# Feed-forward input products as seven half products, narrower matmuls, and a second mixer with wide products

## Chip, cores and metric

One core of a Trainium2 chip. The metric is the device time of one execution in microseconds. Three runs of the kernel before took 1454.93, 1454.94 and 1455.49 us; the time is their median, 1454.94 us.

## The reference

Two layers of a speech encoder over 384 tokens (256 frames of one stream, 16 of each of 8 later streams), width 1024, feed-forward width 2816, all in float32:

```python
def _swiglu(x, w_in, w_down):
    gate, up = jnp.split(x @ w_in, 2, axis=-1)
    return (jax.nn.silu(gate) * up) @ w_down

def _post_norm(x, sub, g, b):
    return _layer_norm(DEEPNORM_ALPHA * x + sub, g, b)

x <- LN(alpha*x + 0.5*SwiGLU_1(x)); x <- LN(alpha*x + Mixer(x)); x <- LN(alpha*x + 0.5*SwiGLU_2(x))
```

The mixer of the first layer is chunked attention with 16 heads and a relative bias; that of the second is windowed attention with 16 query heads on 4 key heads, rotary positions and one learned sink per head, which stands in the denominator of the softmax. There are four feed-forwards, two in each layer.

## The kernel before

**Products in three passes.** A float32 matrix is held as a high part and a remainder, both in the matmul's rounded float32 type: `split` (L68 to L70) casts the high part on ScalarE (L69) and subtracts on VectorE (L70). `mm3` (L119 to L122) multiplies high by high, high by low and low by high, so a product costs three matmuls. The lines L120, L121 and L122 below are these three.

**Weights.** All weights pass once through a ring of 8 tiles of 128x1024 (`ring_h`, `ring_l`), in the order that `Weights` (L72) is given. `ahead` (L97) issues a DMA on SP into a raw tile and splits it as soon as the ring has a free place; `take` hands out the next tile and `done` (L115) frees it. `first` (L78) brings the first four tiles in slabs, while dummy matmuls on zeros (`warm`, L952 to L955) run ahead of the first product.

**Tokens.** `x` holds the tokens in rows; `xh`, `xl` hold them transposed (features on partitions) and split, for three blocks of 128 tokens. `to_xT` (L130) transposes a block on TensorE with `ident` (L134) and splits it out of the bank; `layer_norm` (L145) makes a block of `x`: a sum with the old `x` (L150), statistics (L153), the normalised value (L165 to L169).

**A feed-forward** (`ffn`, L200) goes over 22 chunks of 128 hidden features. `in_chunk` (L211) makes one chunk: a gate tile and an up tile of weights, 8 blocks of 128 input features each, three matmuls for a block, 128 weight columns against all 384 tokens. Then SiLU and product (L208, L209) and the split of the hidden state. After each chunk from the third on, `down` (L271) adds the chunk two before it to the output: 6 steps (3 token blocks by 2 halves of the output) of three matmuls with 512 columns. The last 4 chunks' `down` steps come at the end, block by block, so that the layer norm of a block runs beside the next block's. The first two chunks are special: `opening` (L280) in the first feed-forward, elsewhere `first_chunks` (L229), which takes the tokens as the stationary operand, needs four weight tiles at once, and handles block by block, so that it can start before the last block is normalised. `ffn_order` (L184) lists the weight tiles in this order.

**The mixers** use a small planner, `Flow` (L339), which puts attention units between the products by their length, room in banks and what they need. `Mixer.natural` (L519) makes products with the tokens stationary: `natural(512)` with 512 weight columns, `natural(256)` with 256. In the second mixer (`mixer_b`, L692) there is one product of 512 and four of 256. It loads its sinks (L704, L707) and their negatives (L712, L714) at its own start.

## Time and profile before

| | |
|---|---|
| median of three runs | 1454.94 us |
| the profiled execution: time, span | 1457.14 us, 1455.4 us |
| granted TensorE clock over the span | 0.997 |
| TensorE matmuls (PE) | 1439.5 us, 99%, 8302 matmuls |
| TensorE weight loads (PEld) | 1298.8 us, 89% |
| VectorE (DVE), ScalarE (ACT), GpSimd (POOL) | 683.2, 543.9, 43.9 us |
| data moved by DMA | 203.81 MB, mean 140 GB/s |

How to read it: a busy time is the union of an engine's instruction durations. Matmuls overlap: the profile gives a 384-column matmul 0.34 us, while the next one starts 0.17 us after it, so the price of a matmul in a stream is the distance between starts. The weight load of a matmul is a row of its own (PEld) and runs beside the matmul before. "[5.16 <-DVE x L169]" behind a row means that the engine stood idle for 5.16 us ahead of it, until VectorE's instruction of L169 ended.

### The profile page before, as it was taken

Reading aid. Unit: us, or ns where it says so; the run is one execution under the profiler, and the core shown is the slowest. Engines: PE = TensorE matmul, PEld = TensorE weight load, DVE = VectorE, ACT = ScalarE, POOL = GpSimd, SP = SyncE. Lnnn points to the kernel's source line nnn. Section 1 sums busy time; section 2 is a strip of 40 time slices with the busy share of each in tenths; the row PEclk is TensorE's granted clock in tenths of the full one; section 3 lists DMA queues with packets and bytes.
Section 4 is the critical chain, followed back from the end, with each engine's and each line's share of the span. In section 5 each row is a group of like instructions: output and inputs, shape, how many; then the busy total and the mean of one; then the engine's idle time right before and its main releaser. Section 6 shows DMA issues by size and latency. Waiting matters only on the chain.

```text
span 1455.4 us, 20664 instructions
## 1 busy us (share of the span) xinstructions
PE 1439.5 (99%) x8302; PEld 1298.8 (89%) x8302; DVE 683.2 (47%) x1119; ACT 543.9 (37%) x989; POOL 43.9 (3%) x77
## 2 busy tenths in 40 slices
PE   9999999999999999999999999999899999999997
PEld 8999999897887899999989999999797789999996
DVE  6433333754356633333374333334776674333334
ACT  6333233355564433333323333332256453323320
POOL 0000000100000000000000000000210000000001
PEclk9999999999999999999999999999999999999999
DMA  8733333266845533333334333333441054333321
GB/s 291 273 130 131 118 128 130 95 216 199 274 150 155 186 125 130 130 119 127 130 102 161 129 130 127 120 130 130 148 154 43 15 190 144 130 121 126 131 87 44
DMA packets 69455, 203.81 MB, mean 140 GB/s; under 512 B 7228, under 2 KB 20160, under 8 KB 69232
## 3 DMA queue, kind: packets, MB, share of 16 engines
q1 hardware_dynamic: 63856, 188.24, 38.7%
q0 software_dynamic: 3200, 10.85, 2.3%
q10 hardware_dynamic: 2304, 3.41, 0.6%
q8 instruction: 65, 1.06, 0.3%
q14 instruction: 30, 0.25, 0.1%
HBM read 196.56 MB, written 5.24 MB: 139 GB/s over the span
## 4 chain that ended last, share of the span: by engine, by line
PE 97%; DMA 1%; ACT 1%; DVE 1%; issue 0%; POOL 0%; DVEq 0%; ACTq 0%
PE bank L120 30%; PE bank L122 30%; PE bank L121 30%; PE bank L651 1%; PE bank L134 1%; DMA sinkpb<-in_sinks 1%; PE bank L627 1%; PE bank L893 1%; PE bank L796 0%; PE bank L835 0%; PE bank L453 0%; PE bank L955 0%; PE bank L824 0%; PE bank L426 0%; DMA raw<-in_w_in 0%; PE bank L463 0%
## 5 line engine op out<-in xcount | busy, mean ns | idle before, releaser
L70 DVE TENSOR_TENSOR ring_l<-raw,ring_h 128x1024 fp32r<-128x1024 f32 x312 | 381.3, 1224 | 497.9 <-ACT ring_h L69 497.2
L69 ACT CAST ring_h<-raw 128x1024 fp32r<-128x1024 f32 x312 | 326.7, 1049 | 713.6 <-PE bank L121 417.8
L120 PE MATMUL bank<-xh,ring_h 128*128 128x384 f32 x1440 | 485.1, 337 | 0.0
L122 PE MATMUL bank<-xh,ring_l 128*128 128x384 f32 x1440 | 482.3, 335 | 0.0
L121 PE MATMUL bank<-xl,ring_h 128*128 128x384 f32 x1440 | 481.6, 334 | 0.0
L120 PEld LDWEIGHTS bank<-xh,ring_h 128*128 128x128 f32 x1440 | 270.5, 188 | 5.4 <-issue 1.2
L121 PEld LDWEIGHTS bank<-xl,ring_h 128*128 128x128 f32 x1440 | 270.5, 188 | 3.8 <-DVE xl L70 0.5
L122 PEld LDWEIGHTS bank<-xh,ring_l 128*128 128x128 f32 x1440 | 270.3, 188 | 0.0
L122 PE MATMUL bank<-ring_h,hl 128*128 128x512 f32 x528 | 209.0, 396 | 0.0
L120 PE MATMUL bank<-ring_h,hh 128*128 128x512 f32 x528 | 208.9, 396 | 0.0
L121 PE MATMUL bank<-ring_l,hh 128*128 128x512 f32 x528 | 207.6, 393 | 0.0
L209 DVE TENSOR_TENSOR hf<-sg,bank 128x384 f32<-128x384 f32 (+1 forms) x91 | 49.2, 540 | 182.4 <-PE bank L122 164.2
L120 PE MATMUL bank<-ring_h,xh 128*128 128x512 f32 (+1 forms) x336 | 125.9, 375 | 0.0
L122 PE MATMUL bank<-ring_h,xl 128*128 128x512 f32 (+1 forms) x336 | 122.0, 364 | 0.7 <-DVE ve L157 0.7
L121 PE MATMUL bank<-ring_l,xh 128*128 128x512 f32 (+1 forms) x336 | 121.3, 361 | 0.0
L122 PEld LDWEIGHTS bank<-ring_h,hl 128*128 128x128 f32 x528 | 99.2, 188 | 24.0 <-DVE hl L70 1.0
L121 PEld LDWEIGHTS bank<-ring_l,hh 128*128 128x128 f32 x528 | 99.6, 189 | 19.6
L120 PEld LDWEIGHTS bank<-ring_h,hh 128*128 128x128 f32 x528 | 99.5, 188 | 19.4
L120 PEld LDWEIGHTS bank<-ring_h,xh 128*128 128x128 f32 x336 | 63.7, 190 | 12.8 <-issue 3.5
L122 PEld LDWEIGHTS bank<-ring_h,xl 128*128 128x128 f32 x336 | 63.6, 189 | 11.3 <-DVE ve L157 1.1
L121 PEld LDWEIGHTS bank<-ring_l,xh 128*128 128x128 f32 x336 | 63.8, 190 | 8.1 <-issue 0.2
L159 POOL TENSOR_TENSOR rstd<-ve,mhalf 128x1 f32<-128x1 f32 x18 | 17.6, 979 | 1249.1 <-DVE ve L157 1249.1
(171 smaller groups left out, 805.7 us busy)
## 6 DMA issues: line engine op xcount, KB each, us to landing
raw<-in_w_in SPq DMA_DIRECT2D x172, 512.0 KB, 3.2
raw<-in_w_down SPq DMA_DIRECT2D x88, 512.0 KB, 3.2
kta<-in_kT_a SPq DMA_DIRECT2D x16, 512.0 KB, 6.2
vca<-in_v_a SPq DMA_DIRECT2D x16, 512.0 KB, 5.6
raw<-in_w_qk_a SPq DMA_DIRECT2D x16, 512.0 KB, 3.4
raw<-in_w_v_a SPq DMA_DIRECT2D x8, 512.0 KB, 3.4
raw<-in_w_o_a SPq DMA_DIRECT2D x8, 512.0 KB, 5.9
raw<-in_w_kv_b SPq DMA_DIRECT2D x8, 512.0 KB, 3.7
```

What stands on the lines that cost most here:

```text
L69: nc.scalar.copy(hi, src)
L70: nc.vector.tensor_tensor(lo, src, hi.bitcast(F32), op=ALU.subtract)
L120: nc.tensor.matmul(out, lh, rh, start=first, stop=False)
L121: nc.tensor.matmul(out, lh, rl, start=False, stop=False)
L122: nc.tensor.matmul(out, ll, rh, start=False, stop=last)
L134: nc.tensor.transpose(out=pt[:, j * P:(j + 1) * P], in_=x[:, t, (4 * h + j) * P:(4 * h + j + 1) * P], identity=ident,)
L159: nc.gpsimd.tensor_tensor(rstd, ve, mhalf, op=ALU.pow)
L209: nc.vector.tensor_tensor(hf, sg, up, op=ALU.mult)
L627: nc.tensor.matmul(pk[32 * j:32 * j + 32, 0:n], qbd[:, 4 * g + j, b, :], kt[:, j, :], start=True, stop=True)
L651: nc.tensor.matmul(po[32 * j:32 * j + 32, 0:P], pT[:, w] if i < 2 else pT[0:DS, w], vc[:, i, d] if i < 2 else vn[:, d], start=(i == 0), st ...
L893: nc.tensor.matmul(po[w, i, :], vn[:, b + i, d] if l else vc[:, b + i, d], pT[0:DS, u] if l else pT[:, u], start=(l == 0), stop=(l == 1),)
```

## The change

**Half products.** From the fifth chunk on (18 of 22 in each feed-forward) the two products of a chunk (gate and up, 1024 input features by 384 tokens) are taken as a product of 2 by 2 blocks: weights A11 (gate, first 512 input features), A12 (gate, last 512), A21 and A22 (up); tokens B in first and last 512 features, and in the first and the last 64 tokens of each block of 128. Instead of eight block products of 512 features by 128 hidden features by 192 tokens there are seven (the scheme of Strassen and Winograd), on sums of blocks: S1 = A21 + A22, S2 = S1 + A11, S3 = A11 + A21, S4 = S2 + A12 (plain sums; the signs are in the token combinations and in the factor -1 of `gated_half`). `Chunk.make` forms a sum on VectorE and splits it into a half unit of the ring; `combine` forms the four token combinations of a block of 128 tokens once per feed-forward (`ch`, `cl`), for the first two blocks at the transposes, for the last in `combine_late`, after a GpSimd sum of its two parts. Two banks X and Y of 192 columns collect the products; ScalarE copies three intermediate results out (`kept`), VectorE adds them (`summed`).

**Ring and order.** The ring holds the same bytes in 16 units of 512 columns, a full tile takes two. A chunk in the new form takes seven units. The order of a feed-forward is padded to a multiple of 16 units, 6 here. In a chunk A11, A12, S2, S1, S3, A22, S4 have single down steps between them (`STEPS`), as many as the hidden states made so far allow.

**Small edits.** WARM goes from 3 to 2. `load_sinks` moves the sinks out of `mixer_b`, behind the gate that the ninth chunk of the first feed-forward opens. `mixer_b` makes its keys, values and queries by three products of 512 columns (`w_qkv_b`). The tokens' first transposed copy, `xTf`, lies in the space of `x`.

```diff
-RING = 8
+RING = 16
+UNIT = 512
+PLAIN = 4
+HQ = 64
...
-WARM = 3
+WARM = 2
...
+    ring_h = xp.tile([P, RING, UNIT], F32R, name="ring_h")
+    ring_l = xp.tile([P, RING, UNIT], F32R, name="ring_l")
...
+    class Chunk:
...
+        def make(self, name, hi, lo):
+            def add(out, p, q):
+                nc.vector.tensor_tensor(out, p, q, op=ALU.add)
+            if name == "A11":
+                raw = W.pairs.tile([P, 4, UNIT], F32, name="pair")
+                for s in range(2):
+                    nc.sync.dma_start(raw[:, 2 * s:2 * s + 2, :].rearrange("p a f -> p (a f)"), self.src[s])
+                self.a11, self.a12, self.a21, self.a22 = (raw[:, i, :] for i in range(4))
+                self.s1 = W.pairs.tile([P, UNIT], F32, name="s1")
+                split(self.a11, hi, lo)
+                add(self.s1, self.a21, self.a22)
+            elif name == "A12":
+                split(self.a12, hi, lo)
+                self.s3 = self.a21
+                add(self.s3, self.a11, self.a21)
+            elif name == "S2":
+                self.s2 = self.a11
+                add(self.s2, self.s1, self.a11)
+                split(self.s2, hi, lo)
+            elif name == "S1":
+                split(self.s1, hi, lo)
+            elif name == "S3":
+                split(self.s3, hi, lo)
+            elif name == "A22":
+                split(self.a22, hi, lo)
+            else:
+                add(self.a12, self.s2, self.a12)
+                split(self.a12, hi, lo)
...
+                u = us.start % RING
+                if chunk:
+                    job[0].make(job[1], ring_h[:, u, :], ring_l[:, u, :])
+                elif not isinstance(job, int):
+                    raw = wr.tile([P, 1024], F32, name="raw")
+                    nc.sync.dma_start(raw, job)
...
+            if comb:
+                if h == 0:
+                    xf = comb[0][2].tile([P, KC, P], F32, name="xf")
+                nc.scalar.copy(xf[:, 4 * h:4 * h + 4, :].rearrange("p k q -> p (k q)"), pt)
+        if comb:
+            combine(xf[:, 0:4, :], xf[:, 4:8, :], t)
+        else:
+            late.append(t)
...
+    def combine_late():
+        while late:
+            t = late.pop(0)
+            xf = comb[0][2].tile([P, KC, P], F32, name="xf")
+            nc.gpsimd.tensor_tensor(xf, xh[:, t].bitcast(F32), xl[:, t].bitcast(F32), op=ALU.add)
+            combine(xf[:, 0:4, :], xf[:, 4:8, :], t)
+    def combine(b1, b2, t):
+        ch, cl, _ = comb[0]
+        b11, b12, b21, b22 = b1[:, :, 0:HQ], b1[:, :, HQ:P], b2[:, :, 0:HQ], b2[:, :, HQ:P]
+        nc.vector.tensor_tensor(b11, b11, b12, op=ALU.subtract)
+        nc.vector.tensor_tensor(b12, b22, b12, op=ALU.subtract)
+        nc.vector.scalar_tensor_tensor(b22, b11, -1.0, b22, op0=ALU.mult, op1=ALU.subtract)
+        nc.vector.scalar_tensor_tensor(b21, b22, -1.0, b21, op0=ALU.mult, op1=ALU.subtract)
+        for i, f in enumerate((b11, b22, b12, b21)):
+            split(f, ch[:, i, :, t, :], cl[:, i, :, t, :])
...
+    STEPS = ("A11", "A12", None, "S2", "S1", None, "S3", None, None, "A22", "S4", None)
+    def ffn_plan(layer, which):
...
+            chunk = Chunk((layer, which), w_in[j, 0], w_in[j, 1])
+            left = (n - 2 * NT * (PLAIN - 2)) * (j - PLAIN + 1) // (NF - PLAIN) + 2 * NT * (PLAIN - 2) - set_
+            set_ += left
+            for i, name in enumerate(STEPS):
+                if name:
+                    steps.append((j, (chunk, name)))
+                elif left:
+                    steps.append(next(downs))
+                    left -= 1
+            steps += [next(downs) for _ in range(left)]
...
+        order += [w_down[j] for j in range(NF - NTAIL, NF)]
+        n = sum(1 if isinstance(o, tuple) else 2 for o in order)
+        return order + ([-n % RING] if n % RING else [])
...
+            def chunk_step(j, name):
+                if name == "A11":
+                    hv["x"], hv["y"] = bank()[:, 0:T // 2], bank()[:, 0:T // 2]
+                    hv["hf"] = tp.tile([P, T], F32, name="hf")
+                    hv["sg"] = tp.tile([P, 2, T // 2], F32, name="sg")
+                    hv["up"] = tp.tile([P, T // 2], F32, name="up")
+                    hs[j] = hp.tile([P, T], F32R, name="hh"), hp.tile([P, T], F32R, name="hl")
+                X, Y, sg, up = hv["x"], hv["y"], hv["sg"], hv["up"]
+                hf = halves(hv["hf"])
+                out = Y if name in ("A11", "S2", "S3", "A22") else X
+                wn = W.take()
+                hi, lo = W.half(wn, 0)
+                for k in range(KC // 2):
+                    f = slice(k * P, (k + 1) * P)
+                    if name in ("S1", "S2", "S3", "A22"):
+                        i = ("S1", "S2", "S3", "A22").index(name)
+                        rh, rl = (c[:, i, k].rearrange("p t q -> p (t q)") for c in comb[0][:2])
+                        ov = out
+                    else:
+                        kk, q = (k, 0) if name == "A11" else (k + 4, 0) if name == "A12" else (k + 4, HQ)
+                        rh, rl = (c[:, :, kk, q:q + HQ] for c in (xh, xl))
+                        ov = out.rearrange("p (t q) -> p t q", q=HQ)
+                    mm3(
+                        ov, hi[:, f], lo[:, f], rh, rl, k == 0 and name in ("A11", "A12", "S1"),
+                        k == KC // 2 - 1, partial=True,
+                    )
+                W.done(wn)
+                def kept(name):
+                    b = tp.tile([P, T // 2], F32, name=name)
+                    nc.scalar.copy(b, Y)
+                    hv[name] = b
+                def gated_half(i, u):
+                    nc.vector.scalar_tensor_tensor(
+                        hf[:, i], u.rearrange("p (t q) -> p t q", q=HQ), -1.0,
+                        sg[:, i].rearrange("p (t q) -> p t q", q=HQ), op0=ALU.mult, op1=ALU.mult,
+                    )
+                def summed(out, kept):
+                    nc.vector.tensor_tensor(out, X, hv[kept], op=ALU.add)
+                if name == "A11":
+                    kept("p1")
+                elif name == "A12":
+                    summed(sg[:, 0], "p1")
+                    nc.scalar.activation(sg[:, 0], sg[:, 0], AF.Silu)
+                elif name == "S2":
+                    kept("u2")
+                elif name == "S3":
+                    kept("u3")
+                    summed(up, "u3")
+                elif name == "A22":
+                    gated_half(0, Y)
+                elif name == "S4":
+                    summed(sg[:, 1], "u2")
+                    nc.scalar.activation(sg[:, 1], sg[:, 1], AF.Silu)
+                    gated_half(1, up)
+                    split(hv["hf"], hs[j][0], hs[j][1])
...
+                combine_late()
                 next(fc)
-            for j in range(2, NF):
-                in_chunk(j)
-                if first and j < 2 + NT:
...
+    def load_sinks():
...
+            m.natural(512, take_q, first=True)
+            m.natural(512, take_kv, whole=True)
...
-            for c in (4, 6):
-                acc = m.natural(256)
-                for t in range(NT):
-                    flow.waiting.insert(t, (set(), {"qr": 1}, queries((2, 0, 1)[t], c, acc)))
+            m.natural(512, take_q2, whole=True)
+            for c in range(4, 8):
                 add_p(c)
-                add_p(c + 1)
...
     ffn(0, 0, 0, first=True)
     with tc.issue_after(gate[0]):
+        sunk = load_sinks()
         mixer_a()
     ffn(0, 1, 2)
     ffn(1, 0, 0)
-    mixer_b()
+    mixer_b(sunk)
     ffn(1, 1, 2, final=True)
```

What this moves, at three places. TensorE, between two chunks, before: the last matmuls of an input product and the first of a down step (`hh`, `hl` are the hidden state's two parts).

```order
L120 MATMUL bank<-xh,ring_h 128x384
L121 MATMUL bank<-xl,ring_h 128x384
L122 MATMUL bank<-xh,ring_l 128x384
L120 MATMUL bank<-ring_h,hh 128x512
L121 MATMUL bank<-ring_l,hh 128x512
L122 MATMUL bank<-ring_h,hl 128x512
```

After: the end of A12, a down step, the start of S2 (`ch`, `cl` are the token combinations; L195 to L197 are the lines of `mm3`).

```order
L195 MATMUL bank<-xh,ring_h 128x192
L196 MATMUL bank<-xl,ring_h 128x192
L197 MATMUL bank<-xh,ring_l 128x192
L195 MATMUL bank<-ring_h,hh 128x512
L196 MATMUL bank<-ring_l,hh 128x512
L197 MATMUL bank<-ring_h,hl 128x512
L195 MATMUL bank<-ch,ring_h 128x192 [waits Activation_49]
L196 MATMUL bank<-cl,ring_h 128x192
L197 MATMUL bank<-ch,ring_l 128x192
```

Matmuls of 384 columns have become more matmuls of 192, and a down step stands inside a chunk.

VectorE, in one chunk, before: the product with SiLU, the hidden state's split, the three weight tiles of a chunk (two of `w_in`, one of `w_down`).

```order
L209 TENSOR_TENSOR hf<-sg,bank 128x384 [waits PE_49,Activation_49]
L70 TENSOR_TENSOR ring_l<-raw,ring_h 128x1024 [waits DMAHW1_49,Activation_49]
L70 TENSOR_TENSOR hl<-hf,hh 128x384 [waits Activation_49]
L70 TENSOR_TENSOR ring_l<-raw,ring_h 128x1024 [waits DMAHW2_49,Activation_49]
L70 TENSOR_TENSOR ring_l<-raw,ring_h 128x1024 [waits DMAHW3_49,PE_49,Activation_49]
```

After, the greater part of a chunk (`pair` holds A11 to A22, `s` S1; L86 are the sums, L417 `summed`, L411 `gated_half`, L73 the splits).

```order
L417 TENSOR_TENSOR sg<-bank,p_1459 128x192 [waits PE_49,Activation_49]
L73 TENSOR_TENSOR ring_l<-pair,ring_h 128x512 [waits Activation_49]
L86 TENSOR_TENSOR pair<-pair 128x512 [waits DVE_49]
L73 TENSOR_TENSOR ring_l<-raw,ring_h 128x1024 [waits PE_49,Activation_49]
L73 TENSOR_TENSOR ring_l<-pair,ring_h 128x512 [waits PE_49,Activation_49]
L417 TENSOR_TENSOR up<-bank,u_1519 128x192 [waits Activation_49]
L73 TENSOR_TENSOR ring_l<-pair,ring_h 128x512 [waits Activation_49] x2
L411 SCALAR_TENSOR_TENSOR hf<-bank,sg 128x3x64 [waits PE_49]
L73 TENSOR_TENSOR ring_l<-s_1536,ring_h 128x512 [waits Activation_49]
L86 TENSOR_TENSOR s_1716<-pair 128x512 [waits DMAHW5_49]
L86 TENSOR_TENSOR pair<-pair 128x512 [waits DMAHW4_49,DVE_49]
```

The sums and the reads of the banks now stand in one queue with the splits, and wait for ScalarE and TensorE in turn.

VectorE between the second and the third feed-forward, before: the last block's sum and statistics, and the fifth weight tile of the third feed-forward (`raw_6357`); its first four stand further ahead in the queue.

```order
L150 SCALAR_TENSOR_TENSOR x_80<-x_80,bank_4596 128x512 [waits PE_49]
L70 TENSOR_TENSOR ring_l_84<-raw_6357,ring_h_83 128x1024 [waits DMAHW3_49,Activation_49]
L70 TENSOR_TENSOR xl_82<-bank_6340,xh_81 128x512 [waits Activation_49]
L70 TENSOR_TENSOR xl_82<-bank_6347,xh_81 128x512 [waits Activation_49]
L153 BN_STATS st_6382<-x_80 128x6 [waits DVE_49]
L150 SCALAR_TENSOR_TENSOR x_80<-x_80,bank_4600 128x512 [waits PE_49]
```

After: `raw_8678`, `raw_8685` and `raw_8692` are the second, third and fourth tile of the third feed-forward.

```order
L73 TENSOR_TENSOR ring_l_84<-raw_8678,ring_h_83 128x1024 [waits DMAHW0_49,Activation_49]
L73 TENSOR_TENSOR ring_l_84<-raw_8685,ring_h_83 128x1024 [waits DMAHW4_49,Activation_49]
L73 TENSOR_TENSOR xl_82<-bank_8661,xh_81 128x512 [waits Activation_49]
L73 TENSOR_TENSOR xl_82<-bank_8668,xh_81 128x512 [waits Activation_49]
L253 SCALAR_TENSOR_TENSOR x_80<-x_80,bank_5820 128x512
L253 SCALAR_TENSOR_TENSOR x_80<-x_80,bank_5824 128x512 [waits PE_49]
L256 BN_STATS st_8715<-x_80 128x6 [waits DVE_49] x2
L73 TENSOR_TENSOR ring_l_84<-raw_8692,ring_h_83 128x1024 [waits DMAHW6_49]
L258 BN_AGGR mv_8720<-st_8715 128x2 [waits DVE_49]
```

The first tiles of the next feed-forward stand later in VectorE's queue than they did, the fourth behind the last block's sums and statistics.

## Rows read from the trace of the kernel before

**Rows 1.** The page, busy time of each engine (us, share, instructions).

```profile
PE 1439.5 (99%) x8302; PEld 1298.8 (89%) x8302; DVE 683.2 (47%) x1119; ACT 543.9 (37%) x989; POOL 43.9 (3%) x77
```

**Rows 2.** The page, the chain of waits: shares of the span by engine.

```profile
PE 97%; DMA 1%; ACT 1%; DVE 1%; issue 0%; POOL 0%; DVEq 0%; ACTq 0%
```

**Rows 3.** Timeline of PE, one chunk (start, duration in us, what).

```profile
525.86 0.39 PE L120 MATMUL bank<-ring_h,hh 128*128 128x512 f32 x1
...
530.04 0.34 PE L120 MATMUL bank<-xh,ring_h 128*128 128x384 f32 x1
...
538.39 0.39 PE L120 MATMUL bank<-ring_h,hh 128*128 128x512 f32 x1
```

**Rows 4.** Timeline of PE, wide and narrow products in the second mixer.

```profile
1040.65 0.39 PE L120 MATMUL bank<-ring_h,xh 128*128 128x512 f32 x1
...
1042.69 0.39 PE L120 MATMUL bank<-ring_h,xh 128*128 128x512 f32 x1
...
1080.64 0.28 PE L122 MATMUL bank<-ring_h,xl 128*128 128x256 f32 x1
...
1096.12 0.28 PE L122 MATMUL bank<-ring_h,xl 128*128 128x256 f32 x1
```

**Rows 5.** Timeline of PEld, the first loads after transposes, in both mixers.

```profile
407.72 0.19 PEld L120 LDWEIGHTS bank<-xh,ring_h 128*128 128x128 f32 x1
407.83 0.19 PEld L121 LDWEIGHTS bank<-xl,ring_h 128*128 128x128 f32 x1
...
1062.97 0.19 PEld L120 LDWEIGHTS bank<-ring_h,xh 128*128 128x128 f32 x1
1063.08 0.19 PEld L121 LDWEIGHTS bank<-ring_l,xh 128*128 128x128 f32 x1
```

**Rows 6.** Costliest groups, DVE, shapes apart (count | busy us, mean ns | idle before).

```profile
L70 DVE TENSOR_TENSOR ring_l<-raw,ring_h 128x1024 fp32r<-128x1024 f32 x312 | 381.3, 1224 | 497.9 <-ACT ring_h L69 497.2
L70 DVE TENSOR_TENSOR hl<-hf,hh 128x384 fp32r<-128x384 f32 x82 | 45.1, 550 | 1.2 <-ACT hh L69 1.2
L70 DVE TENSOR_TENSOR ring_l<-slabs,ring_h 128x512 fp32r<-128x512 f32 x7 | 4.8, 692 | 1.5 <-ACT ring_h L69 1.2
L734 DVE TENSOR_TENSOR qr<-bank,cs 128x256 f32<-128x256 f32 x9 | 3.8, 419 | 1.6 <-PE bank L748 1.4 <-PE bank L773 0.2
```

**Rows 7.** The same view, ACT.

```profile
L69 ACT CAST ring_h<-raw 128x1024 fp32r<-128x1024 f32 x312 | 326.7, 1049 | 713.6 <-PE bank L121 417.8 <-PE bank L122 217.4 <-issue 33.8
L69 ACT CAST hh<-hf 128x384 fp32r<-128x384 f32 x82 | 41.7, 508 | 8.8 <-DVE hf L209 8.5
L69 ACT CAST xh<-bank 128x512 fp32r<-128x512 f32 x30 | 16.8, 586 | 54.3 <-PE bank L134 53.8
L69 ACT CAST xh<-bank 128x256 fp32r<-128x256 f32 x10 | 3.7, 372 | 5.3 <-PE bank L835 5.2
```

**Rows 8.** Timelines: DVE after the first mixer, PE between the middle feed-forwards.

```profile
457.69 1.38 DVE L150 SCALAR_TENSOR_TENSOR x<-x,bank 128x512 f32<-128x512 f32 x2 [1.23 <-PE bank L122]
458.99 1.28 DVE L153 BATCH_NORM_STATS2 st<-x 128x6 f32<-128x512 f32 x2
...
753.26 0.39 PE L122 MATMUL bank<-ring_h,hl 128*128 128x512 f32 x1
753.49 0.39 PE L120 MATMUL bank<-ring_h,xh 128*128 128x512 f32 x1
```

**Rows 9.** Timelines of DVE and PE, start of the second mixer.

```profile
1046.56 0.17 DVE L714 TENSOR_SCALAR nsinkpb<-sinkpb 128x8 f32<-128x8 f32 x1 [3.79 <-DMA sinkpb<-in_sinks]
...
1048.46 0.87 PE L134 MATMUL bank<-ident,x 128*128 128x128 f32 x3 [5.16 <-DVE x L169]
```

**Rows 10.** Timelines of PEld and DVE, the program's start.

```profile
5.04 0.34 PEld L955 LDWEIGHTS bank<-warm 128*128 128x128 f32 x1 [0.52 <-issue]
...
6.74 0.30 PEld L121 LDWEIGHTS bank<-xl,ring_h 128*128 128x128 f32 x1 [0.52 <-DVE xl L70]
...
5.51 0.56 DVE L70 TENSOR_TENSOR ring_l<-slabs,ring_h 128x384 fp32r<-128x384 f32 x1 [1.06 <-ACT ring_h L69]
```

More of the change, by code (lines that the diff above doesn't have):

```diff
@@ L70, in split, with __init__ @@
         nc.vector.tensor_tensor(lo, src, hi.bitcast(F32), op=ALU.subtract)
+    class Chunk:
+        names = ("A11", "A12", "S2", "S1", "S3", "A22", "S4")
+        def __init__(self, ffn, gate, up):
+            self.ffn, self.src = ffn, (gate, up)
+        def make(self, name, hi, lo):
[26 more added lines that the diff above has]
+                split(self.a12, hi, lo)
@@ L200, in ffn @@
     def ffn(layer, which, n, first=False, final=False):
-        with tc.tile_pool(name="hp", bufs=NTAIL + 2) as hp, tc.tile_pool(name="tp", bufs=2) as tp:
+        with ExitStack() as pools:
+            hp = pools.enter_context(tc.tile_pool(name="hp", bufs=NTAIL + 2))
+            tp = pools.enter_context(tc.tile_pool(name="tp", bufs=2))
+            cp = pools.enter_context(tc.tile_pool(name="cp", bufs=1))
+            W.pairs = pools.enter_context(tc.tile_pool(name="pairs", bufs=2))
+            W.ffn = (layer, which)
+            comb[:] = [[cp.tile([P, 4, KC // 2, NT, HQ], F32R, name=n) for n in ("ch", "cl")] + [cp]]
+            if first:
+                start_up(tp)
             gb = None if first else load_gb(layer, n)
@@ L304, in ffn @@
                 fc = first_chunks()
+                combine_late()
                 next(fc)
-            for j in range(2, NF):
-                in_chunk(j)
-                if first and j < 2 + NT:
+            wd = {}
+            for step in ffn_plan(layer, which):
+                if len(step) == 3:
+                    j, t, h = step
+                    if j not in wd:
+                        wd[j] = W.take()
+                    down(j, wd[j], t, h)
+                    if t == NT - 1 and h == 1:
+                        W.done(wd[j])
+                    continue
+                j, job = step
+                if job:
+                    chunk_step(j, job[1])
+                    if job[1] != "S4":
+                        continue
+                else:
+                    in_chunk(j)
+                if first and j == 2:
+                    for t in range(NT):
+                        combine(*(xTf[:, i:i + 4, t * P:(t + 1) * P] for i in (0, 4)), t)
+                if first and PLAIN <= j < PLAIN + NT:
                     with tc.issue_after(hold(hs[j])):
-                        nc.gpsimd.dma_start(x[:, j - 2, :], a["x"][j - 2])
+                        nc.gpsimd.dma_start(x[:, j - PLAIN, :], a["x"][j - PLAIN])
                 if first and j == 8:
@@ L314, in ffn @@
                     next(fc)
[L315 to L320 removed]
+            comb.clear()
             ws = {j: W.take() for j in range(NF - NTAIL, NF)}
@@ L547, in natural @@
                 W.done(ws[i])
-            return acc
+            for t in range(NT):
+                each(t, acc[t])
     def mixer_a():
```

238 lines of the change are left out of this document (132 added, 106 removed).

## Prediction, made before the changed kernel was run

> **What bounds the kernel now.** Read the page's busy table first. TensorE is busy for 1439.5 of 1455.4 us, VectorE for 47% of the span [rows 1]. The chain of waits says the same: 97% of it is TensorE [rows 2]. So a change is worth what it takes off TensorE's stream, and what it makes TensorE wait for. TensorE's own rows give the price of one matmul by its width. In an input chunk 48 matmuls of 384 columns take 538.39 - 530.04 = 8.35 us, 0.174 us each; the 18 matmuls of 512 columns of the down projection before them take 530.04 - 525.86 = 4.18 us, 0.232 each [rows 3]. In the mixers, 512 columns take 2.04 / 9 = 0.227 us and 256 columns 15.48 / 129 = 0.120 us [rows 4]. From 256 to 512 columns one column costs 0.107 / 256 = 0.00042 us, and a fixed 0.013 us comes on top. The next thing to see is the weight load that goes with every matmul. It normally starts when the matmul before it starts, and hides. Where the matmul before it is short it can be seen alone: after the transposes the load for L120 starts at 407.72 and the next load, which can only start when L120 itself has taken its weights, at 407.83, and the pair at 1062.97 and 1063.08 shows the same [rows 5]. A load of 128 float32 columns thus occupies its path for 0.11 us, under all widths that the kernel uses today (0.120 and up). That is the number on which this change turns.
>
> **The half products, 72 chunks (18 in each of four feed-forwards).** A chunk had 48 matmuls of 384 columns; it gets 7 x 4 x 3 = 84 of 192 columns. The columns fall by an eighth, the weight loads rise by three quarters. No row has 192 columns, so the price is bounded from both sides. From below: the line through the wider rows, 0.120 - 64 x 0.00042 = 0.093 us. From above: the nearest width in the trace, 256 columns, 0.120 us. I take 0.11, the row of the load, since 0.093 is under it and a matmul can't start before its weights are in. Then a chunk takes 84 x 0.11 = 9.24 us for 8.35: +0.89 us, times 72 = **+64 us**. At the lower end it is 7.84 us, 72 x -0.51 = -37 us; at the upper end 10.08, 72 x 1.73 = +125 us.
>
> The Trainium skill (TensorE: Matmul & The Clock Gate, LDWEIGHTS (loading the stationary operand)) speaks against the change too: it sets a load's time by its columns alone, P / 1.2 ns, which is 0.107 us for 128 columns, an estimate from that page. By it a chunk would take 8.96 us, the term would be +44 us and the whole 1502 us. The rows' 0.11 is 3% above that rule.
>
> **What hides beside it.** VectorE gets the most new work. Per chunk: seven splits of 512 columns and four sums of 512 at 0.69, 0.89 of a 1024 split at 1.22, five half-width operations of 192 columns at about 0.35 (0.42 for 256, 0.69 for 512, so 0.0011 less for each column fewer), one split of 384 at 0.55 [rows 6]: 4.83 + 2.76 + 1.09 + 1.75 + 0.55 = 11.0 us. ScalarE: 7 x 0.59 + 0.93 + 5 x 0.32 + 0.51 = 7.2 us (0.32 from 0.37 for 256 columns and 0.59 for 512 in the same way) [rows 7]. TensorE's period is 9.24 plus 5.33 down steps of 3 x 0.232, 3.7, so 12.9 us. VectorE is hidden at 85%, and costs nothing as long as its queue keeps up at the two banks that all seven products share. The tightest place: X must be read (the sum after A12) before S1 writes it. From the end of A22 VectorE has a half gate, three rows of 0.69, a sum, a split, a half gate, the wait for ScalarE's 0.51, the 0.55 split, two rows of 0.69 and that sum: 6.6 us. TensorE meanwhile has S4, a down step, A11, A12, a down step and S2: 4 x 1.32 + 2 x 0.70 = 6.7 us. It just fits, so I put 0, with an upper end of 0.5 us a chunk, 36 us. The combinations of the tokens (12 sums and 12 splits a feed-forward) fall beside first products, chunks 2 and 3 and 12 down steps, some 40 us of TensorE: 0.
>
> **The ends of the feed-forwards.** The ring keeps its size, but the padding to a multiple of 16 takes 6 of 16 half units from the loads ahead. Today the first four weight tiles of the next stage are all split before the last down step; now only one is. With T the end of the down steps, ScalarE's three casts of 1.05 run from T - 2.1 to T + 1.05, then two of the token tile end at T + 2.3, VectorE's two splits behind them at T + 2.9; then stand two sums and two statistics of the layer norm (2.7 us), and only then the split of the fourth tile, 1.22, at T + 6.8 [rows 6, 7, 8]. Between the second and third feed-forward the first product reads all four tiles at once: TensorE has two matmuls (0.45) and waits **6.3 us**, where it now goes on without a gap [rows 8]. A mixer takes the tiles one by one and needs the fourth about 4.4 us after T: **2.5 us** each at two mixers. Sum +11.3 us, ends 0 (the scheduler's cover is better than I read it) and 20.
>
> **The small edits.** The sinks: VectorE stands at the loads of them, at the start of the second mixer (3.79 us at the last), with the layer norm's last step behind it, and TensorE waits 5.16 us for that step [rows 9]. Loaded during the first feed-forward they are there 900 us early: **-5.2 us**; what is late next is the 2.5 us counted above. Wide products: 288 matmuls of 256 columns, 34.6 us, become 144 of 512, 32.7: **-1.9 us**. One dummy matmul less: two passes, whose loads start (6.74 - 5.04) / 2 = 0.85 us apart. The first product's second matmul, which loads at 6.74, could then load at 5.0 [rows 10], but the split for its second to fourth tiles ends at 6.07 and that of the next slab later, so about 0.6 us is lost again: **-1.1 us** (0 to -1.7; +1.7 if the clock then rises later).
>
> **Sum.** 64 + 11.3 - 5.2 - 1.9 - 1.1 = +67 us on the profiled execution's 1457.1 us. The median of the runs, 1454.9 us, stands 2.2 us under it, and gives **1522 us**. About 0.2% (2.9 us) is what a measurement here can tell from no change.
>
> **Rivals.**
> 1. *The load doesn't bind* (faster). If a load could run ahead of the matmul before it, a narrow matmul would cost what its columns cost, 0.093 us. For it: in steady streams no load is ever the last to end. Against it: the 0.11 us of the loads seen alone. Place: the 84 matmuls of each chunk; it decides below (8.35 - 3.1/72) / 84 = 0.099 us a matmul. VectorE would then be at 11.0 of 11.5 us, and the X bank would come up to 0.7 us late in a chunk (5.9 us of TensorE against 6.6), less where neighbouring rows overlap; I put 5 us in all. Time: -37 + 11.3 - 8.2 + 5 = -29, 1426 us.
> The Trainium skill has a rule for a stream without weight loads (same page, Back-to-back issue gap): N / 2.4 + 2.5 ns, 0.0825 us for 192 columns, 6.9 us a chunk, about 100 us less, an estimate. The rows don't follow it: for 384 columns it gives 0.163 where they show 0.174.
> 2. *Load and fixed part add up*: 0.120 us, as at 256 columns, whose rows can't tell the one from the other. 1455 + 125 + 3 = 1583 us.
> 3. *VectorE sets the pace*: its 11.0 us and the waits in line with it (cast of a down tile 1.05, hidden state 0.51, copy of the third sum 0.35, some 0.7 for results) come to 13.6 us a chunk, 0.7 over TensorE's 12.9: +46 us more, 1568 us.
> 4. *The change doesn't do what it says*, its matmuls not fewer columns: the instruction lists show 84 rows of 192 columns a chunk, so nothing for it.
>
> **Chances and range.** Forecast 0.58, rival 1 0.20, rival 2 0.08, rival 3 0.10, and 0.04 for a price near 0.099 us, which would leave the time where it was. The forecast's own range is 1495 to 1552 (down to the skipped end stalls, up to VectorE's half of its upper end). To hold 8 in 10 it has to reach rival 1: 1418 to 1552; rival 2 and most of rival 3 lie outside. Faster 0.20, same 0.04, slower 0.76.
>
> **What would show it.** In the new profile: starts of consecutive 192-column matmuls 0.11 us apart and weight loads back to back; 12.9 us from one chunk's A11 to the next; TensorE still over 95% busy, VectorE near 75%; one gap of some 6 us between the middle feed-forwards, none for the sinks. Starts 0.093 apart would make the forecast wrong by its main term; gaps before S1 with VectorE as releaser would mean rival 3.

## The result, and the profile after

The changed kernel takes **1870.23 us** (median of 4 runs, 1867.48 to 1882.54) against 1455.22 us of the kernel before, a ratio of 1.2864 with a 95% interval of 1.2842 to 1.2885. Forecast were 1522 us and a range up to 1552. The sign was right, the size was wrong by a factor of six. The profiled execution took 1882.54 us, its span is 1880.7.

The page of the changed kernel, busy times, granted clock by slices of the span, and shares of the chain:

```profile
PE 1653.6 (88%) x10748; PEld 1472.3 (78%) x10748; DVE 1130.4 (60%) x2140; ACT 789.2 (42%) x1693; POOL 58.5 (3%) x81
...
PEclk9898898999998998899899988999998999889889
...
PE 29%; DVE 8%; DMA 7%; issue 3%; ACT 2%; SPq 0%; POOL 0%; DVEq 0%; ACTq 0%; POOLq 0%
```

Against [rows 1, 2]: TensorE is no longer busy all the time, and its granted clock, 0.997 over the span before, is 0.923 and below nine tenths in 15 of the 40 slices. VectorE is busy for 60%, so it isn't short of time on the average. The chain's shares add up to half of the span only; behind TensorE it names VectorE and a transfer.

Where the 425 us of the span went, by stage (from the start of the first to the start of the last down matmul of each feed-forward in TensorE's timeline, and what lies between):

| | before | after | small edits only | both cures | cures, no low parts |
|---|---|---|---|---|---|
| first feed-forward | 252.5 | 351.4 | 251.3 | 291.2 | 275.3 |
| first mixer | 216.4 | 226.8 | 218.5 | 232.5 | 234.9 |
| second feed-forward | 252.5 | 352.9 | 251.4 | 291.9 | 275.0 |
| between second and third | 26.4 | 35.2 | 31.3 | 39.6 | 39.2 |
| third feed-forward | 252.5 | 345.4 | 251.6 | 290.3 | 273.1 |
| second mixer | 164.8 | 185.3 | 168.8 | 184.0 | 190.2 |
| fourth feed-forward | 250.4 | 344.4 | 250.4 | 288.4 | 271.0 |

(The last three columns are runs of the next section.) Of the 425 us, 386 lie in the feed-forwards and 40 at the mixers and between the middle feed-forwards. By kind: TensorE's idle time is 218.1 us for 6.8; the distances between matmul starts that exceed the full-clock price of their width without idle time come to 151.7 us for 21.0; and the matmuls at full-clock price to 1501.5 for 1418.1. So waiting is +211 us, the lower clock about +131, and the price itself about +83, near the +64 of the forecast. The last two depend on the price that one takes for a width, and can shift by some 15 us from one to the other; the waiting doesn't.

Timeline of TensorE, changed kernel, one chunk (start, duration, what, wait):

```profile
700.16 0.27 PE L195 MATMUL bank<-ch,ring_h 128*128 128x192 f32 x1
...
701.72 0.27 PE L197 MATMUL bank<-ch,ring_l 128*128 128x192 f32 x1
...
709.87 0.27 PE L197 MATMUL bank<-xh,ring_l 128*128 128x192 f32 x1
713.39 0.53 PE L195 MATMUL bank<-xh,ring_h 128*128 128x192 f32 x1 [3.25 <-DVE sg L417]
713.72 0.42 PE L196 MATMUL bank<-xl,ring_h 128*128 128x192 f32 x1
713.93 0.41 PE L197 MATMUL bank<-xh,ring_l 128*128 128x192 f32 x1
```

Fourteen steps lie between 700.16 and 701.72, **0.111 us** for a matmul of 192 columns, against the 0.11 forecast from [rows 5]. Then A11 ends, and A12 waits 3.25 us for VectorE's read of its bank, the sum `sg` of L417; behind that wait the steps are 0.21 us. What VectorE did in that time, and SP's queue:

```profile
705.53 0.68 DVE L73 TENSOR_TENSOR ring_l<-pair,ring_h 128x512 fp32r<-128x512 f32 x1
...
707.34 0.69 DVE L73 TENSOR_TENSOR ring_l<-pair,ring_h 128x512 fp32r<-128x512 f32 x1 [0.18 <-ACT ring_h L72]
711.65 0.69 DVE L86 TENSOR_TENSOR s<-pair 128x512 f32<-128x512 f32 x1 [3.62 <-DMA pair<-in_w_in]
712.38 0.69 DVE L86 TENSOR_TENSOR pair<-pair 128x512 f32<-128x512 f32 x1
712.99 0.35 DVE L417 TENSOR_TENSOR sg<-bank,u 128x192 f32<-128x192 f32 x1
```

```profile
706.24 1.02 SPq L91 DMA_DIRECT2D pair<-in_w_in  x2
```

VectorE stood at the sum S1 of a later chunk, which waits for the transfer of that chunk's gate and up tile. SP had issued it at 706.24, just after VectorE's split of 705.53 had ended (the last out of the buffer that the tile goes into), and 5.4 us before VectorE could go on. The read of the bank, 0.35 us of work for which TensorE waited, stood two instructions behind. Over the whole kernel the group of S1 sums (count | busy us, mean ns | idle before):

```profile
L86 DVE TENSOR_TENSOR s<-pair 128x512 f32<-128x512 f32 x72 | 49.8, 692 | 236.5 <-DMA pair<-in_w_in 236.1
```

236.1 / 72 = 3.3 us a chunk. TensorE's own waits show who stood behind: the first group below holds the matmuls of A11, A12, S4 and of the plain chunks, the second those of S1, S2, S3 and A22 (behind the last bar: the idle time before them, and what ended most of it).

```profile
L195 PE MATMUL bank<-xh,ring_h 128*128 128x192 f32 (+1 forms) x1152 | 363.6, 316 | 147.7 <-DVE sg L417 67.3
L195 PE MATMUL bank<-ch,ring_h 128*128 128x192 f32 x1152 | 326.4, 283 | 39.1 <-DVE sg L417 19.8
```

Together that is 187 of TensorE's 218 us. The clock in the same place, by stretches of 1 us (busy us and count of PE, PEld, DVE, ACT, POOL, then the granted clock, DMA share, GB/s):

```profile
711.00:712.00 1.00, 0.00 (x0) 0.00 (x0) 0.35 (x1) 0.00 (x0) 0.00 (x0) 1.00 0.01 4
712.00:713.00 1.00, 0.00 (x0) 0.00 (x0) 0.96 (x3) 0.00 (x0) 0.00 (x0) 0.50 0.00 0
...
714.00:715.00 1.00, 1.00 (x6) 1.00 (x6) 0.42 (x2) 0.73 (x2) 0.00 (x0) 0.50 0.00 0
...
719.00:720.00 1.00, 1.00 (x12) 1.00 (x11) 0.00 (x0) 0.51 (x1) 0.00 (x0) 1.00 0.52 102
```

During the wait the clock falls to 0.50, that is 1.2 GHz, and is full again only by 719: 6 matmuls in a microsecond instead of about 11. The Trainium skill describes this (TensorE: Matmul & The Clock Gate, HAM oscillation — how this bites in real kernels): matmul groups with a wait for a transfer between them each start at the low clock. The trace agrees for most of the waits, though TensorE's wait is for VectorE: of its 44 waits of more than 2.5 us 39 were followed by matmuls at half clock. There are 53 stretches at half clock in all, 294 us, 5.5 us each in the mean.

The ends of the stages, TensorE at the start of the third feed-forward and of the second mixer, and a weight load at the program's start:

```profile
968.98 0.80 PE L196 MATMUL bank<-ring_l,xh 128*128 128x512 f32 x1 [5.43 <-DVE ring_l L73]
...
1365.21 1.08 PE L1007 MATMUL bank<-ident,qr 128*128 128x128 f32 x4 [9.99 <-issue]
...
5.03 0.34 PEld L196 LDWEIGHTS bank<-xl,ring_h 128*128 128x128 f32 x1 [0.52 <-DVE ring_l L73]
```

The first is the wait forecast at 6.3 us. The second begins 12 us behind the last down matmul, where the sinks' 5.16 us began 11 us behind it [rows 9], and is twice as long; but it is a wait at the transposes of the queries, not of the tokens. ScalarE and VectorE stand there for a tile of the mixer's weights, and what makes the queries stands behind it in VectorE's queue:

```profile
1358.39 1.04 ACT L72 CAST ring_h<-raw 128x1024 fp32r<-128x1024 f32 x1 [7.29 <-DMA raw<-in_w_qkv_b]
1359.47 1.23 DVE L73 TENSOR_TENSOR ring_l<-raw,ring_h 128x1024 fp32r<-128x1024 f32 x1 [5.49 <-ACT ring_h L72]
```

The third is the row that was expected at 5.0 [rows 10]. One more wait, at the end of the first mixer, where the second feed-forward transposes its last tokens, was not forecast at all:

```profile
584.19 1.94 PE L209 MATMUL bank<-ident,x 128*128 128x128 f32 x8 [4.13 <-DVE x L272]
```

VectorE's layer norm of these tokens stands there behind a token combination (L241), a sum of the next feed-forward and a split of 3.43 us, for 1.23 elsewhere, which runs beside GpSimd's sum for `combine_late`:

```profile
569.69 3.43 DVE L73 TENSOR_TENSOR ring_l<-raw,ring_h 128x1024 fp32r<-128x1024 f32 x1
573.04 0.41 DVE L241 TENSOR_TENSOR xf<-xf 128x256 f32<-128x256 f32 x1
573.38 0.68 DVE L86 TENSOR_TENSOR pair<-pair 128x512 f32<-128x512 f32 x1
```

### The profile page after: what moved, and what is told of

The parts are those of the page before. It is cut to its first block, busy times and chain, and to the rows that moved or that the text cites. A ratio compares the mean times of both kernels' runs of the same rounds, so it can differ in the third digit from the quotient of the medians.

```text
span 1880.7 us, 27401 instructions
## 1 busy us (share of the span) xinstructions
PE 1653.6 (88%) x10748; PEld 1472.3 (78%) x10748; DVE 1130.4 (60%) x2140; ACT 789.2 (42%) x1693; POOL 58.5 (3%) x81
## 3 DMA queue, kind: packets, MB, share of 16 engines
q10 hardware_dynamic: 2304, 3.41, 0.5%
## 5 line engine op out<-in xcount | busy, mean ns | idle before, releaser
L195 PE MATMUL bank<-xh,ring_h 128*128 128x192 f32 (+1 forms) x1152 | 363.6, 316 | 147.7 <-DVE sg L417 67.3
L195 PEld LDWEIGHTS bank<-xh,ring_h 128*128 128x128 f32 x1152 | 243.0, 211 | 165.9 <-DVE sg L417 70.7
L72 ACT CAST ring_h<-pair 128x512 fp32r<-128x512 f32 x432 | 265.1, 619 | 248.2 <-PE bank L196 180.5
L195 PE MATMUL bank<-ch,ring_h 128*128 128x192 f32 x1152 | 326.4, 283 | 39.1 <-DVE sg L417 19.8
L197 PE MATMUL bank<-xh,ring_l 128*128 128x192 f32 (+1 forms) x1152 | 357.9, 311 | 0.1
L196 PE MATMUL bank<-xl,ring_h 128*128 128x192 f32 (+1 forms) x1152 | 357.3, 310 | 0.0
L73 DVE TENSOR_TENSOR ring_l<-pair,ring_h 128x512 fp32r<-128x512 f32 x432 | 294.3, 688 | 89.9 <-ACT ring_h L72 87.2
L196 PE MATMUL bank<-cl,ring_h 128*128 128x192 f32 x1152 | 327.9, 285 | 0.0
L197 PE MATMUL bank<-ch,ring_l 128*128 128x192 f32 x1152 | 326.5, 283 | 0.0
L73 DVE TENSOR_TENSOR ring_l<-raw,ring_h 128x1024 fp32r<-128x1024 f32 (+2 forms) x178 | 212.9, 1199 | 167.1 <-ACT ring_h L72 162.8
L195 PEld LDWEIGHTS bank<-ch,ring_h 128*128 128x128 f32 x1152 | 234.5, 204 | 59.2 <-DVE sg L417 20.8
L197 PEld LDWEIGHTS bank<-xh,ring_l 128*128 128x128 f32 x1152 | 244.3, 212 | 0.6 <-DVE ring_l L73 0.4
L196 PEld LDWEIGHTS bank<-cl,ring_h 128*128 128x128 f32 x1152 | 233.2, 202 | 9.7
L197 PEld LDWEIGHTS bank<-ch,ring_l 128*128 128x128 f32 x1152 | 232.2, 202 | 0.0
L195 PE MATMUL bank<-ring_h,hh 128*128 128x512 f32 x528 | 227.1, 430 | 0.0
L197 PE MATMUL bank<-ring_h,hl 128*128 128x512 f32 x528 | 218.8, 414 | 0.0
L86 DVE TENSOR_TENSOR s<-pair 128x512 f32<-128x512 f32 x72 | 49.8, 692 | 236.5 <-DMA pair<-in_w_in 236.1
L197 PEld LDWEIGHTS bank<-ring_h,hl 128*128 128x128 f32 x528 | 105.5, 200 | 26.2 <-DVE hl L73 1.0
L195 PE MATMUL bank<-ring_h,xh 128*128 128x512 f32 x288 | 120.9, 421 | 1.4 <-ACT xh L72 1.4
```

Of the source, the lines that this page charges most:

```text
L72: nc.scalar.copy(hi, src)
L73: nc.vector.tensor_tensor(lo, src, hi.bitcast(F32), op=ALU.subtract)
L86: nc.vector.tensor_tensor(out, p, q, op=ALU.add)
L195: nc.tensor.matmul(out, lh, rh, start=first, stop=False, skip_group_check=partial)
L196: nc.tensor.matmul(out, lh, rl, start=False, stop=False, skip_group_check=partial)
L197: nc.tensor.matmul(out, ll, rh, start=False, stop=last, skip_group_check=partial)
```

## Experiments

The theories: **W**, VectorE's in-order queue stands at a sum that waits for a late transfer; **V**, VectorE's own work sets the pace (the prediction's third rival); **N**, narrow matmuls by themselves bring the clock down.

### A third pair buffer

```diff
-raw = W.pairs.tile([P, 4, UNIT], F32, name="pair")
+raw = W.pairs.tile([P, 4, UNIT], F32, name="pair", bufs=3)
...
-wr = ctx.enter_context(tc.tile_pool(name="wr", bufs=3))
+wr = ctx.enter_context(tc.tile_pool(name="wr", bufs=2))
```

(and one buffer each for `up` and `p1`, to make room.)

> The changed kernel with three buffers for the raw gate and up tiles of a chunk instead of two; to make room, two raw buffers for the other weights instead of three, and one buffer each for two small results. Theory W (VectorE's queue stands at the sum S1, which waits for a transfer that is issued only when the buffer of two chunks before is free, 236 us in all): the transfer is issued about a chunk earlier, VectorE's wait for it falls from 236 us to under 80, TensorE's idle time from 218 to under 100, its granted clock rises from 0.92 to over 0.97, and the time to 1500 to 1650 us. Theory V (VectorE's own work sets the pace, with casts and reads in line): its work is the same, so the time stays within 40 us of 1870. Theory N (narrow matmuls by themselves bring the clock down): the clock stays below 0.95 even where the gaps have gone.

Measured: 1709.24 us, ratio 1.1738 (1.1721 to 1.1756). The control with the small pools and two pair buffers:

> Control for the run before: the changed kernel with two raw buffers for the other weights and one buffer each for two small results, but the two pair buffers it had. All theories: 1870 us within 20; VectorE's wait for the pair near 236 us. If it is off by more, the smaller pools matter and the run with three pairs has to be read against this one.

It took 1885.38 us, 1.2943 (1.2919 to 1.2966): the small pools cost 15 us by themselves, and VectorE's wait was 237.8 us. With the third buffer:

```profile
L86 DVE TENSOR_TENSOR s<-pair 128x512 f32<-128x512 f32 x72 | 51.5, 715 | 52.7 <-DMA pair<-in_w_in 51.5
```

The wait fell by 186 us, TensorE's idle time from 224.0 in the control to 119.9, the time by 176. V is out as the main cause: VectorE's work is the same, 1131.7 us for 1130.4. But W promised under 100 us idle, a clock over 0.97 and at most 1650; clock 0.960 and 1709 say that this transfer wasn't the only thing that came late.

### The waiting sums on GpSimd

```diff
-add(self.s1, self.a21, self.a22)
+nc.gpsimd.tensor_tensor(self.s1, self.a21, self.a22, op=ALU.add)
...
-add(self.s3, self.a11, self.a21)
+nc.gpsimd.tensor_tensor(self.s3, self.a11, self.a21, op=ALU.add)
```

> The changed kernel with the first two of a chunk's four sums (S1 = A21 + A22, S3 = A11 + A21), which wait for the transfer of the pair, on GpSimd instead of VectorE. Buffers and transfers stay as they are. Theory W: what hurts is that reads of the banks and splits stand behind these sums in VectorE's queue; with the wait moved to an idle engine TensorE's idle time falls from 218 us to under 90, the clock rises over 0.97, and the time goes to 1500 to 1620 us. Theory V: VectorE has 1.4 us of 11 less per chunk, so at most 72 x 1.4 = 100 us less, 1770 to 1870. If the transfer is simply too late for TensorE's next product, wherever the wait stands, the time stays above 1800.

Measured: 1672.93 us, 1.1486 (1.1457 to 1.1516), clock 0.972, idle 102.7 us. There are as many buffers for the transfers as in the changed kernel, and the wait simply stands elsewhere (group on GpSimd):

```profile
L95 POOL TENSOR_TENSOR s<-pair 128x512 f32<-128x512 f32 x72 | 94.4, 1311 | 896.6 <-DMA pair<-in_w_in 744.1 <-DVE hf L411 88.8 <-DVE ring_l L73 27.4
```

GpSimd can stand 744 us at the transfer, and the kernel still gains. The gain of 197 us is twice what V allows (100 us), so it was the place of the wait in VectorE's queue that hurt. But the idle time (under 90 was expected) and the time, by 53 us, are again above W's range.

### Both cures

> Both cures at once: three pair buffers (with the smaller pools of that run) and the sums S1 and S3 on GpSimd. The two alone took 161 and 197 us off 1870. If both removed the same wait (the transfer that VectorE stands for), together they give no more than the better one, 1640 to 1675 us, and what is left is another wait: ScalarE's copy of a first product standing behind a cast that waits for VectorE's sum. If the waits were different ones the gains add up, to about 1510 to 1560. Clock 0.97 to 0.99.

Measured: 1660.19 us, 1.1426 (1.1383 to 1.1469), idle 74.7 us, clock 0.965 (0.97 to 0.99 was expected). The cures don't add up: it was one wait. What is left sits in two places of each feed-forward. From A11 to the next A11 most chunks take 12.86 us (some 13.6) with five down steps and 13.55 with six; but the second after a start (in the first feed-forward the first too), the tenth and the eleventh take 16 to 19. ScalarE's, then VectorE's and TensorE's rows at one of them:

```profile
68.30 1.14 ACT L72 CAST ring_h<-pair 128x512 fp32r<-128x512 f32 x2 [1.23 <-DVE pair L86]
69.34 0.31 ACT L407 COPY p<-bank 128x192 f32<-128x192 f32 x1
```

```profile
67.58 0.68 DVE L86 TENSOR_TENSOR pair<-s,pair 128x512 f32<-128x512 f32 x1
68.95 3.41 DVE L73 TENSOR_TENSOR ring_l<-pair,ring_h 128x512 fp32r<-128x512 f32 x2 [0.69 <-ACT ring_h L72]
```

```profile
69.71 0.42 PE L195 MATMUL bank<-ch,ring_h 128*128 128x192 f32 x1 [1.63 <-ACT p L407]
```

S2 may not go on in the bank before ScalarE has copied A11's product out of it. That copy stands behind a cast which waits for VectorE's sum, which stands behind VectorE's splits. The last VectorE row shows one more thing, which the second cure brought with it: two splits take 3.41 us, 0.69 each elsewhere. GpSimd makes S1 and S3 at that time, and over the run these splits take 828 ns in the mean, for 688 in the changed kernel (GpSimd's rows, then the group):

```profile
68.84 1.28 POOL L95 TENSOR_TENSOR s<-pair 128x512 f32<-128x512 f32 x1
70.20 1.61 POOL L99 TENSOR_TENSOR pair<-pair 128x512 f32<-128x512 f32 x1
...
L73 DVE TENSOR_TENSOR ring_l<-pair,ring_h 128x512 fp32r<-128x512 f32 x432 | 353.5, 828 | 81.4 <-ACT ring_h L72 78.8
```

So part of what is left may come from the cure itself; no run shows how much.

Between 142 and 146 us, in a stretch without such waits, the clock is full though the matmuls are narrow, so N is wrong at 192 columns (the next run shows it over whole feed-forwards):

```profile
142.00:146.00 4.00, 4.00 (x31) 3.69 (x30) 3.03 (x4) 1.99 (x5) 0.40 (x1) 1.00 0.00 0
```

### Without the low parts

`Chunk.make` with ScalarE's cast only instead of `split`, on top of both cures.

> As the run with both cures, but leaving out VectorE's subtraction for the low parts of the half units (seven a chunk, 4.8 us of VectorE; the low parts keep what stood in the ring, so the remainders of these weights are not computed). TensorE's instructions and the casts stay. Theory Q (what is left are answers that come late because VectorE's and ScalarE's queues are full between two products): TensorE's idle time falls under 40 us, the clock is over 0.985, and the time is the price of the matmuls alone, 1455 + 72 x 1.02 = 1528 us, plus up to 40 us at the stage ends: 1530 to 1570. Theory P (TensorE waits for the fixed hand-overs, one engine after the other, whatever VectorE's load): over 1600.

Measured: 1597.43 us, 1.0968 (1.0943 to 1.0993), clock 0.982, idle 49.6 us: between the two theories. In the feed-forwards Q holds: nearly all chunks take 12.86 or 13.55 us, a few 13.6 to 14.4, no stretch between the first and the last down step of a feed-forward is at half clock, and a feed-forward is 20.6 to 22.8 us longer than before, where the price alone makes 18 x (84 x 0.1114 - 8.35) = 18.1. The splits that GpSimd's sums held up are among those left out, so the run can't tell full queues from splits that take longer. What was underestimated in Q's figure is the rest: mixers and the stretch between feed-forwards are 57 us longer than before.

### The price of a narrow matmul

Each matmul of 192 columns as one of 128 and one of 64, with the same weights loaded for each. The two ranges don't add up to the changed kernel's products; only the times are read.

> The changed kernel with each half product's matmul of 192 columns as two, of 128 and of 64, with the same weights loaded for each: 168 matmuls a chunk. If the load of 128 weight columns sets the price of a narrow matmul, all are 0.11 us apart, as at 192 columns; a chunk's half products take 168 x 0.11 = 18.7 us. If the price went on falling with the columns, they would be 0.067 and 0.040 us apart by the slope of the wide ones, 9.0 us a chunk, no longer than now. The time is 2100 to 2500 us in the first case and near 1870 in the second.

Measured: 3430.15 us (one run). TensorE's rows in a stretch at full clock, 64 columns and 128:

```profile
60.23 0.28 PE L196 MATMUL bank<-cl,ring_h 128*128 128x64 f32 x1
60.34 0.28 PE L197 MATMUL bank<-ch,ring_l 128*128 128x64 f32 x1
...
60.60 0.27 PE L196 MATMUL bank<-cl,ring_h 128*128 128x128 f32 x1
60.71 0.27 PE L197 MATMUL bank<-ch,ring_l 128*128 128x128 f32 x1
```

0.11 us for both widths, as for 192. What the three widths have in common is the load of 128 weight columns, which sets the price, as the prediction took it; no run loads fewer columns for these products, so that it isn't another fixed cost of a matmul is argued. The Trainium skill's rule for that load (TensorE: Matmul & The Clock Gate, LDWEIGHTS (loading the stationary operand)) gives 0.107 us, 3% under these rows. The time misses its range, 2100 to 2500, for another reason, told below.

### The small edits

The changed kernel with all chunks in the plain form and no token combinations:

> The changed kernel with every chunk in the plain form (48 matmuls of 384 columns), no token combinations: what is left is the ring in half units with its padding, one dummy matmul less, the early sinks and the wide products of the second mixer. By the prediction's terms: sinks -5.2, wide products -1.9, dummy -1.1, ends of the feed-forwards up to +11.3 (padding alone may cost less here: the plain chunks leave the ring other places), so 1447 us if the ends cost nothing and 1458 if they cost what was predicted. All theories of the half products agree on this one; it tells what the rest of the change is worth.

Measured: 1462.59 us, 1.004 (1.0024 to 1.0055): 6 us slower than before, and above both figures. The table shows it at the mixers and between the feed-forwards, which are 11 us longer. So the edits were tried alone, on the kernel before:

> The kernel before with nothing but the sinks loaded early, behind the gate in the first feed-forward. The prediction's term: TensorE's wait of 5.16 us at the second mixer's start goes, 1451 us against 1456 of the kernel before on this chip. Rival: the caches and the layer norm's rows, which stood behind the sinks in GpSimd's queue, start 4 us earlier and collide with the weights there, and the gain is lost: 1456 or more.

> The kernel before with two dummy matmuls instead of three. The prediction's term: -1.1 us (0 to -1.7), 1455 against 1456; if the clock rises later, up to +1.7.

> Both small edits on the kernel before. If the terms add up: -6.3 us, 1450. A version that beats both kernels if the sinks' term holds.

> The kernel before with nothing but the second mixer's wide products: three products of 512 columns, 144 matmuls of 512 for 288 of 256. The prediction's term: -1.9 us, 1454.5 against 1456.4. Rival, from the run with the small edits only, in whose second mixer TensorE ran at half clock for about 13 us beside attention units: the wide products move the attention's short matmuls together, the clock falls, and the time is 5 to 9 us longer, 1461 to 1465.

| edit, on the kernel before | us | ratio, 95% interval |
|---|---|---|
| sinks early | 1450.82 | 0.9956 (0.9943 to 0.9970) |
| one dummy less | 1455.33 | 0.9994 (0.9985 to 1.0002) |
| both | 1449.08 | 0.9951 (0.9938 to 0.9963) |
| wide products | 1458.45 | 1.0021 (1.0012 to 1.0030) |

**Sinks and one dummy less, 1449.08 us, beats both kernels**, the one before by 0.5%. With the sinks early TensorE's transposes in the second mixer begin without the 5.16 us of [rows 9]:

```profile
1042.48 0.60 PE L134 MATMUL bank<-ident,x 128*128 128x128 f32 x4
```

The wide products cost 2.7 us instead of saving 1.9. Their rows show new waits of TensorE among the attention units (first and third of them):

```profile
1098.18 0.50 PE L120 MATMUL bank<-ring_h,xh 128*128 128x512 f32 x1 [1.31 <-ACT xh L69]
...
1143.99 0.44 PE L847 MATMUL bank<-pTp,vb 128*64 128x256 f32 x2 [1.14 <-ACT pTp L839]
```

The rival given there, a lower clock, doesn't explain it: this profile's clock is 0.998.

The run with the small edits holds more than these: the padded ring and the changed order. If the terms add up, the sinks, the dummy and the wide products make -3.8 us, and the rest cost some 10 us without any half products, near the 11.3 us that were forecast for the ends.

And the sinks in the changed kernel:

> The changed kernel with the sinks loaded at the start of the second mixer, as in the kernel before. If the early sinks are worth their 5.5 us there too: 1875. Rival: in the changed kernel TensorE waits 10 us at that place for weights that come late beside the caches, which no longer stand behind the sinks in GpSimd's queue; then late sinks cost nothing or give something back: 1860 to 1870.

Measured: 1873.12 us, 1.2863 (1.2844 to 1.2883), the same as the changed kernel; the second mixer takes 184.5 us by the measure of the table, 185.3 there. With late sinks TensorE waits 5.90 and 6.81 us at that place, with early ones 9.99 once: the 5.5 us can be had only where the weights behind them are in time. That the caches' earlier transfers delay those weights is likely (they run in the same stretch) but wasn't tried apart.

## Why the prediction was wrong

**The step that failed** is the one on VectorE: "VectorE is hidden at 85%, and costs nothing as long as its queue keeps up [...] so I put 0, with an upper end of 0.5 us a chunk". The work was sized well: seven splits of 0.69, four sums of 0.69, a share of 1.24 for the down tile, five reads of 0.35 and a split of 0.56 make 11.0 us, as forecast. What was left out is what that work waits for. The sums S1 and S3 have no ring place to wait for, so the order puts them ahead of bank reads, and they read a raw tile whose transfer SP issues only when the buffer of two chunks before is free. VectorE stood there for 3.3 us a chunk, against room of 0.1 us (6.7 less 6.6) by the prediction's own count of the tightest place. The transfer was part of the moved step and wasn't counted. Nor was the place that it counted, X before S1, where most was lost: TensorE waited 19.8 us at S1 for the sum after A12, and 67.3 us at A12 for the same kind of sum after the S4 of the chunk before.

**The clock had no term.** The prediction priced waits at their length. Here most waits of about 3 us brought half clock for some 5 us behind them: about +131 us on +211 of waiting.

**The third rival was the right engine with the wrong mechanism.** It put VectorE's pace at 13.6 us a chunk and the time at 1568. Its 11.0 us of work plus casts were not the limit: a third buffer took 161 us away with the same work. But it was not all wrong: leaving out the low parts took another 16 us off each feed-forward (291 to 275), though some of these splits took longer there beside GpSimd's sums.

**The main term was right.** 0.11 us forecast, 0.111 measured; a chunk of 12.9 us forecast, 12.86 and 13.55 (13.1 in the mean) measured wherever nothing is late. +64 us became +73 (4 x 18.1). Rivals 1 and 2 are out: no width below 192 is cheaper, and the price isn't 0.120. So even with every wait cured this form of the product is slower here.

**The ends** were +11.3 us forecast, and the mixers and the stretch between came out 40 us longer (10.4, 8.8 and 20.5). The 6.3 us at the third feed-forward were 5.43. The two mixers at 2.5 each went another way: at the start of the first TensorE waits less than 1 us, at the start of the second 9.99, for weights that came late. And the prediction put the combinations of the tokens at 0, while a combination, a sum and a slow split stand ahead of the layer norm where the second feed-forward begins, and TensorE waits 4.13 us there; at the fourth it waits 2.70 and 1.17 at the same transposes. Without half products, in the run with the small edits only, these waits are not there.

**The small edits**: sinks -5.2 forecast, -5.5 measured alone, and nothing in the changed kernel, where "what is late next" was 10 us and not 2.5; dummy -1.1 forecast, -1.0 measured alone, with an interval that includes none; wide products -1.9 forecast, +2.7 measured: the second mixer's products did take 2.0 us less, 102.7 for 104.7, but attention's matmuls took 1.8 more and new waits stand among them.

## What to carry to other kernels

When work is moved onto an engine that is half idle, count not only its busy time but, for each instruction added, what it waits for and who stands behind it in the same queue; one early sum that waited for a transfer cost some 200 of the 415 us here. Put such an instruction on an engine that nobody waits for, or issue its transfer a step earlier: the two cures gave back 197 and 161 us. Then look at whether the two engines slow each other, as VectorE's splits beside GpSimd's sums did here. And price a wait of TensorE at more than its length, since the clock after it is part of the bill.

## What the runs showed of the hardware

The run with 128 and 64 columns ran most of its feed-forwards at half clock with TensorE hardly ever idle (31.7 us of 3428, none of it over 0.3 us between the start and the first fall of the clock). Its windows, early and later (columns as above):

```profile
58.00:62.00 4.00, 4.00 (x34) 3.86 (x34) 1.99 (x3) 0.69 (x2) 0.00 (x0) 1.00 0.01 4
300.00:320.00 20.00, 20.00 (x89) 19.42 (x90) 6.21 (x11) 3.63 (x8) 0.00 (x0) 0.50 0.01 2
```

Theory N, wrong at 192 columns, holds in this run: a stream of loads with short matmuls between them, back to back, lost the clock without a wait (0.628 over the run, 0.213 us a matmul at half clock for 0.11). The loads' rows too are longer then, 0.33 us for 0.19. So halving a matmul's columns once, to 192, cost only the load's price; dividing it again cost the clock as well.

VectorE's splits out of a pair took 0.69 us alone and 1.3 us in the mean where they ran beside a sum on GpSimd, 96 of the 432 in the run with both cures. That the two engines hold each other up is the plain reading; no run was made for it.
